# Seven products of quarters in place of eight, for half of K of sixteen products, and a merge that goes branch by branch

## The chip, the core and the metric

The kernel runs on one core of one Trainium2 chip. The metric is the time of one execution on the device, in microseconds (us). The core has a matrix engine (TensorE, PE in the rows), three engines for elementwise work (VectorE, DVE; ScalarE, ACT; GpSimd, POOL) and an engine that here only starts transfers (SyncE, SP). Each works through its own queue in order. They share an on-chip memory of 128 partitions. Matrix products land in PSUM, eight banks of 128x512 numbers of 4 bytes.

## The reference, cut to what is computed

One layer of a decoder for 256 positions and a model width D of 2048, in single precision:

```
h    = rms_norm(x, norm_mix_g)
proj = h @ w_in                # 2048 x 14336: q k v xr gr sc_b sc_c sc_x g_pre
y_a  = attention(q, k, v) @ w_attn_o        # each branch is 1024 wide
y_b  = rg_lru(xr, gr)     @ w_lru_o
y_c  = short_conv(sc_b, sc_c, sc_x) @ w_sc_o
g_a, g_b, g_c = sigmoid(g_pre + gate_b)     # the gates, 3 x 2048 columns
x    = x + (g_a*y_a + g_b*y_b + g_c*y_c) @ w_out
h    = rms_norm(x, norm_mlp_g)
x    = x + square(relu(h @ w_mlp_up)) @ w_mlp_down    # 2048 -> 8192 -> 2048
out  = rms_norm(x, final_g)
```

## The kernel before

**Numbers in two parts.** Each factor of a product is held as `hi`, the number rounded to the format of the matrix engine, and `lo`, the rest. A product is hi times hi, hi times lo and lo times hi, so every 128 rows of K cost three passes.

**Weights.** They come as 552 units of 256 rows of K by 512 columns (512 KB), one for each job. `fetch` (L133) has SP start the transfer into one of RAW = 5 buffers. `in_parts` (L138) has ACT write `hi` (L141) and DVE write `lo` = raw - hi (L142), each 128x1024, into one of WB = 6 slots. `ahead` (L145) is called before each job for the jobs up to LOOK = 3 further on. A slot comes free when PE has finished the job that reads it, so the conversion of a later job begins there.

**Two kinds of product.** `group` (L219) keeps the weights in the array and streams the activations; it serves the projections xr, qk, sc, sx, sb, gr and the first MLP product up. Its chunk is two units, 32 matmuls, of which 16 (L228) stream only 256 columns. `pair` (L247) keeps the activations in the array and streams 512 columns of weights; it serves v, the gates gt, the branch products y, the output projection wo and the second MLP product dn. A pair makes four PSUM tiles, (row tile t, column group i), each 128x512. With K of 2048 it has 16 jobs, two column groups of eight units, and a job is 12 matmuls (2 row tiles, 2 halves of the unit, 3 passes, L266). A pair of dn covers a quarter of K of that product, and its name gives the part and the pair: dn10 is part 1, pair 0. The name gt21 is the third branch, second pair.

**What lies beside.** A generator given to `beside` (the attention, L537; the second norm) emits its next step at each `a_bit` (L209), which `group` calls once per chunk and `pair` once per two jobs. A group or pair leaves the rest of its evacuation in `after`, one piece of which goes out per `a_bit`. `finish` emits all that is left.

**Order.** SP runs in the order of the program. The queues of PE, ACT, DVE and POOL are set by a scheduler when the kernel is built. The list of weights (L104) must be in the order in which the products are called: sc, sx, sb, gr with the attention steps spread over them, one per chunk, then gt and y in turn for three branches, two pairs each, then wo, then four parts of up and dn.

**Buffers.** `block` gives tiles of 128x512 out of NBLK = 59. Six PSUM banks (`bank`) serve groups and pairs, two (`small`) serve transposes and the attention. In the attention each head h makes `lg` (logits), `pp` (transposed weights of the softmax, copied to `pT` by ACT at L561) and `po` (values), and all three take a small bank.

The kernel already has a branch for seven products in `pair` and in `ahead`, but with every NB_ constant at 0 it makes no jobs of that kind.

Of the kernel before, what the change touches and what calls it, by code (L numbers as in the profile page):

```python
# [7 lines left out]
F32 = mybir.dt.float32  # L8
# [4 lines left out]
P = 128  # L13
# [23 lines left out]
NBLK = 59  # L37
RAW = 5
WB = 6
# [4 lines left out]
NB_V = NB_GATE = NB_Y = NB_OUT = NB_DOWN = 0  # L44


def as_sequence(nu, nb):

    n1, n2 = ([("n", 0, 0, i, u) for u in range(4 * nb // 2, nu)] for i in range(2))
    if not nb:  # L50
        return n1 + n2
    s = {m: [("s", m, b, 0, 0) for b in range(nb)] for m in range(1, 8)}
    h = len(n1) // 2
    return s[1] + s[2] + s[3] + n2[:h] + s[4] + n2[h:] + s[5] + n1[:h] + s[6] + n1[h:] + s[7]
# [3 lines left out]
def trunk_kernel(ctx, tc, x8, xn, pv, rows, w_in, rel, onehot, w_a, lru_w, w_l, w_s, w_out, w_up, w_down, out2):  # L58
# [27 lines left out]
    def h_mixed(b, k, m):  # L86
        raise NotImplementedError
# [18 lines left out]
    order += [("ws", w_in, g, 0, 8, 0) for g in (12, 13, 14, 15, 10, 11, 8, 9)]  # L106
    for br, w in enumerate((w_a, w_s, w_l)):
# [86 lines left out]
    side, after = [], []  # L194

# [23 lines left out]
    def group(name, w, g, acts, evac):  # L219

        nk = follow("ws", w, g)
        ps = [bank(f"{name}_{j}") for j in range(4)]
        rest = []

        def block_product(j, k, hi, lo, kk):
            cs = slice(j * P, (j + 1) * P)
            pe.matmul(ps[j], hi[:, kk, cs], acts[k], start=(k == 0), stop=False)  # L227
            pe.matmul(ps[j][:, :S], lo[:, kk, cs], acts[k][:, :S], start=False, stop=(k == nk - 1))  # L228

        for k0 in range(0, nk, 4):  # L230
            u = used[0]
            used[0] += 2
            ahead(u + 1 + LOOK)
            if u < 2:
                for k in range(k0, k0 + 4):
                    for j in range(4):
                        block_product(j, k, *parts[u + (k - k0) // 2], k % 2)
            else:
                for j in range(4):
                    for k in range(k0, k0 + 4):  # L240
                        block_product(j, k, *parts[u + (k - k0) // 2], k % 2)
                    if k0 + 4 == nk:
                        rest.append(evac(j, ps[j]))
            a_bit()
        after.extend(r for r in rest if r)

    def pair(name, w, g, plain, mixed, evac):  # L247


# [20 lines left out]
        def copied(key, what):  # L270
            r = block(f"{name}{what}")
            act.activation(r, ps[key], AF.Copy)
            got[what] = r

        def summed(what):
            r = block(f"{name}{what}")
            dve.tensor_add(r, ps[1, 0], got["r1"])
            got[what] = r

        others = {(0, 0): (None, None), (0, 1): ("x", OP.subtract), (1, 0): ("r1", OP.add), (1, 1): ("z", OP.add)}  # L280
        for n, s in enumerate(seq):
# [10 lines left out]
            else:  # L292
# [3 lines left out]
                if b == nb - 1:  # L296
                    if m == 1:
                        copied((0, 0), "r1")
                    elif m == 2:
                        copied((0, 1), "r5")  # L300
                    elif m == 3:
                        summed("x")
                    elif m == 4:
                        summed("y")
                        z = block(f"{name}z")
                        dve.tensor_sub(z, got["r5"], got["y"])
                        got["z"] = z
# [227 lines left out]
    pair("v", w_in, 4, lambda k, t: in_two(hl[k], t), h_mixed, evac)  # L535
# [76 lines left out]
    for gidx in range(2):  # L612
        def evac(j, ps, gidx=gidx):
            g = 4 * gidx + j
            b = total(ps, f"sb{g}")
            dve.tensor_mul(b, b, rsb)
            dve.tensor_mul(b, b, half(sc, g))
            o = block(f"C{g}", F32R)
            split(o, b)
            C.append(o)  # L620
        group(f"sb{gidx}", w_in, 10 + gidx, hl, evac)


    for gidx in range(2):
        def evac(j, ps, gidx=gidx):
            g = 4 * gidx + j
            y = total(ps, f"gr{g}")

            def rest():
                dve.tensor_mul(y, y, rsb)  # L630
                z = u256(f"gz{g}")
                act.activation(z, y, AF.Square)
                act.activation(z, z, AF.Copy, scale=0.044715, bias=1.0)
                pool.tensor_mul(z, z, y)
                act.activation(z, z, AF.Tanh, scale=math.sqrt(2.0 / math.pi))
                dve.scalar_tensor_tensor(y, z, 1.0, y, op0=OP.add, op1=OP.mult)
                dve.scalar_tensor_tensor(y, half(hh, g), 0.5, y, op0=OP.mult, op1=OP.mult)
                o = block(f"B{g}", F32R)
                split(o, y)
                B.append(o)  # L640
            return rest
        group(f"gr{gidx}", w_in, 8 + gidx, hl, evac)
# [76 lines left out]
    for p2 in range(2):  # L719
# [28 lines left out]
        pair(f"wo{p2}", w_out, 2 * p2, m_plain, None, evac)  # L748
# [16 lines left out]
    for part in range(PARTS):  # L765
        U = []
        for gidx in range(4):
            def evac(j, ps):
                b = total(ps, f"up{part}{gidx}{j}")
                dve.scalar_tensor_tensor(b, b, 0.0, b, op0=OP.max, op1=OP.mult)  # L770
                o = block(f"U{part}{gidx}{j}", F32R)
                split(o, b)
                U.append(o)
            group(f"up{part}{gidx}", w_up, 4 * part + gidx, h2, evac)
# [5 lines left out]
        for p2 in range(2):  # L780
# [12 lines left out]
            pair(f"dn{part}{p2}", w_down, 2 * p2, lambda k, t: in_two(U[k], t), None, evac)  # L793
# [77 lines left out]
```

## Time and profile before

| | |
|---|---|
| median of 3 executions | 1610.56 us (1610.06 to 1612.92) |
| the profiled execution: own time | 1611.42 us |
| the profiled execution: span of the trace | 1609.7 us |
| mean granted clock of TensorE | 0.997 |
| PE busy | 1582.9 us, 98% of the span |
| DVE busy | 958.4 us, 60% |
| ACT busy | 760.8 us, 47% |
| chain of work that ended last | PE 97% |

The busy time of an engine is a sum over stages with different limits, so the shares say which engine to look at, not what a change is worth. For PE the chain of waits gives what the work costs without a gap. For the engines beside it the question is stage by stage whether they are done in time, and for that the timeline of DVE and ACT is read, from the start of one instruction to the start of the next where they stand close.

### The profile page before, as it was taken

The numbers are of one execution on the slowest core, as the hardware profiler recorded it, in microseconds if no ns is written. First come the engines' busy times: TensorE is split into PE (matmuls) and PEld (weight loads), VectorE is DVE, ScalarE is ACT, GpSimd is POOL, SyncE is SP. The second block draws the span as 40 slices with busy tenths as digits, with TensorE's granted clock in tenths as the row PEclk, the third lists the DMA queues.
The fourth block names the chain that finished last, engine by engine and source line by source line (L and its number), as shares of the span: only waits on it lengthen the run. The fifth ranks groups of instructions, "written<-read, shape, count | busy, mean of one in ns | idle before, by whom it ended". The sixth has DMA issues, their size and how long they took to land.

```text
span 1609.7 us, 20538 instructions
## 1 busy us (share of the span) xinstructions
PE 1582.9 (98%) x7886; PEld 1338.5 (83%) x7886; DVE 958.4 (60%) x1237; ACT 760.8 (47%) x1026; POOL 74.8 (5%) x85
## 2 busy tenths in 40 slices
PE   6999999999999999999999999999999999999996
PEld 5888888888888888888888888888888888888885
DVE  8865566776655565555655566555654655556553
ACT  5545845556544444344445554344433444344442
POOL 6021200001100000000000000000000000000000
PEclk9999999999999999999999999999999999999998
DMA  7665465555756665765655556655656556655662
GB/s 256 223 206 168 145 219 170 173 171 183 243 191 195 221 195 192 237 201 184 194 184 185 176 187 196 192 186 186 194 191 209 184 183 200 200 183 184 197 195 65
DMA packets 86418, 307.65 MB, mean 191 GB/s; under 512 B 10141, under 2 KB 10405, under 8 KB 86320
## 3 DMA queue, kind: packets, MB, share of 16 engines
q1 hardware_dynamic: 82656, 296.57, 57.4%
q0 software_dynamic: 2656, 8.45, 1.8%
q10 hardware_dynamic: 1008, 1.32, 0.3%
q8 instruction: 61, 1.00, 0.3%
q14 instruction: 37, 0.30, 0.1%
HBM read 304.20 MB, written 2.11 MB: 190 GB/s over the span
## 4 chain that ended last, share of the span: by engine, by line
PE 97%; DVE 1%; DMA 1%; ACT 0%; issue 0%; ACTq 0%; SPq 0%; DVEq 0%
PE dn L266 22%; PE gt L266 16%; PE up L227 15%; PE y L266 8%; PE up L228 8%; PE wo L266 5%; PE qk L227 4%; PE v L266 3%; PE qk L228 2%; PE sb L227 2%; PE sc L227 2%; PE sx L227 2%; PE gr L227 2%; PE xr L227 1%; PE sc L228 1%; PE sb L228 1%
## 5 line engine op out<-in xcount | busy, mean ns | idle before, releaser
L142 DVE TENSOR_TENSOR lo<-raw,hi 128x1024 fp32r<-128x1024 f32 x552 | 671.8, 1229 | 571.9 <-ACT hi L141 571.7
L141 ACT ACTIVATE hi<-raw 128x1024 fp32r<-128x1024 f32 x552 | 575.3, 1057 | 701.7 <-PE dn L266 193.1
L227 PE MATMUL up<-h,hi 128*128 128x512 f32 x1024 | 362.1, 399 | 0.0
L266 PE MATMUL dn<-hi,U 128*128 128x512 f32 x1024 | 316.2, 389 | 0.0
L228 PE MATMUL up<-h,lo 128*128 128x256 f32 x1024 | 287.9, 281 | 0.0
L266 PE MATMUL gt<-hi,h 128*128 128x512 f32 x768 | 238.0, 390 | 0.0
L227 PEld LDWEIGHTS up<-h,hi 128*128 128x128 f32 x1024 | 192.6, 188 | 47.6
L266 PEld LDWEIGHTS dn<-hi,U 128*128 128x128 f32 x1024 | 192.3, 188 | 40.0
L266 PE MATMUL dn<-lo,U 128*128 128x512 f32 x512 | 199.4, 389 | 0.0
L228 PEld LDWEIGHTS up<-h,lo 128*128 128x128 f32 x1024 | 193.8, 189 | 0.1
L266 PEld LDWEIGHTS gt<-hi,h 128*128 128x128 f32 x768 | 144.2, 188 | 29.9
L266 PE MATMUL gt<-lo,h 128*128 128x512 f32 x384 | 149.5, 389 | 0.0
L266 PEld LDWEIGHTS dn<-lo,U 128*128 128x128 f32 x512 | 96.1, 188 | 19.7
L227 PE MATMUL qk<-h,hi 128*128 128x512 f32 x256 | 91.5, 401 | 0.0
L266 PEld LDWEIGHTS gt<-lo,h 128*128 128x128 f32 x384 | 72.1, 188 | 14.8
L228 PE MATMUL qk<-h,lo 128*128 128x256 f32 x256 | 71.8, 280 | 0.0
L227 PEld LDWEIGHTS qk<-h,hi 128*128 128x128 f32 x256 | 48.1, 188 | 12.1 <-ACT hi L141 0.6
L227 PE MATMUL xr<-h,hi 128*128 128x512 f32 x128 | 46.0, 410 | 7.7 <-DVE h L349 7.6
L266 PE MATMUL wo<-hi,MH 128*128 128x512 f32 x128 | 50.2, 392 | 0.0
L266 PE MATMUL wo<-hi,ML 128*128 128x512 f32 x128 | 49.9, 390 | 0.0
L266 PE MATMUL wo<-lo,MH 128*128 128x512 f32 x128 | 49.8, 389 | 0.0
L228 PEld LDWEIGHTS qk<-h,lo 128*128 128x128 f32 x256 | 48.4, 189 | 0.3
(752 smaller groups left out, 1772.8 us busy)
## 6 DMA issues: line engine op xcount, KB each, us to landing
raw<-in_w_in SPq DMA_DIRECT2D x222, 512.0 KB, 4.3
raw<-in_w_up SPq DMA_DIRECT2D x128, 512.0 KB, 4.0
raw<-in_w_down SPq DMA_DIRECT2D x128, 512.0 KB, 4.2
raw<-in_w_out SPq DMA_DIRECT2D x32, 512.0 KB, 3.6
raw<-in_w_a SPq DMA_DIRECT2D x16, 512.0 KB, 4.4
raw<-in_w_s SPq DMA_DIRECT2D x16, 512.0 KB, 4.3
raw<-in_w_l SPq DMA_DIRECT2D x16, 512.0 KB, 4.3
gb<-in_rows POOLq DMA_DIRECT2D x12, 256.0 KB, 5.0
```

Source lines behind the costliest of these rows:

```text
L141: act.activation(hi, raw, AF.Copy)
L142: dve.tensor_sub(lo, raw, hi.bitcast(F32))
L227: pe.matmul(ps[j], hi[:, kk, cs], acts[k], start=(k == 0), stop=False)
L228: pe.matmul(ps[j][:, :S], lo[:, kk, cs], acts[k][:, :S], start=False, stop=(k == nk - 1))
L266: pe.matmul(ps[key], hl_[x], w2[y][:, kk], start=key not in begun, stop=end and i == 2, skip_group_check=True)
```

## The change

Two constants of `as_sequence` are set: NB_GATE = NB_OUT = NB_DOWN = 2. In the 16 pairs of gt (6), wo (2) and dn (8), units 0 to 3 of K (half of it) are computed by Strassen's scheme: the activations and the weights are cut into quarters, and seven products of sums of quarters replace eight products of quarters. Two blocks b of K, of 512 rows each, share the products' banks. Such a pair has 22 jobs: 14 of kind "s" with 6 matmuls each (products m1 to m7, for b = 0 and 1) and 8 of kind "n" as before. A DVE add in place makes the sum of weight quarters for m2, m3, m4 and m6, and each of the 14 "s" jobs gets its own hi and lo. The sums of activation quarters are made once: for h (`h_sums`, beside the attention), for m (in the rest of gt2/y2, with copies `mf`), and for U of the first two groups of each part (`rest` of up). Products m2, m1, m3 and m4 meet in DVE operations (`step`, L302 and L303) that write two more blocks.

The order of the jobs in a pair is m1, m1, n, m2, m2, n, m3, m3, n, m4, m4, n (of the second column group), then m5, n, m5, m6, n, m6, m7... with the n of the first. A pair uses five banks, since m2 gets its own, (2,0).

The stages are reordered: sc, sx, gt0 and y0, sb, gt1 and y1, gr, gt2 and y2, wo. The attention runs beside sc and sx alone, three steps per `a_bit` (`pace[0] = 3`). `finish` is called before every gate pair and y pair. RAW goes from 5 to 9, WB from 6 to 5, NBLK from 59 to 55.

The number of instructions by queue: PE 7829 before and 7637 after, DVE 1232 and 1696, SP 574 both, POOL 90 both.

```diff
-NBLK = 59
-RAW = 5
-WB = 6
+NBLK = 55
+RAW = 9
+WB = 5
...
-NB_V = NB_GATE = NB_Y = NB_OUT = NB_DOWN = 0
+NB_V, NB_Y = 0, 0
+NB_GATE, NB_OUT, NB_DOWN = 2, 2, 2
...
+    def mixed(ms, ns):
+        ss = [("s", m, b, 0, 0) for m in ms for b in range(nb)]
+        out = []
+        for i, n in enumerate(ns):
+            out += ss[len(ss) * i // len(ns):len(ss) * (i + 1) // len(ns)] + [n]
+        return out
+
+    return mixed((1, 2, 3, 4), n2) + mixed((5, 6, 7), n1)
...
+    def sums(name, a1, a2):
+
+        c = block(f"{name}c")
+        c4 = [c[:, i * P:(i + 1) * P] for i in range(4)]
+        dve.tensor_sub(c4[0], a1[:, P:], a2[:, P:])
+        dve.tensor_sub(c4[1], c4[0], a1[:, :P])
+        dve.tensor_sub(c4[2], a1[:, :P], a1[:, P:])
+        dve.tensor_add(c4[3], a2[:, :P], c4[1])
+        hi, lo = block(f"{name}ch", F32R), block(f"{name}cl", F32R)
+        act.activation(hi, c, AF.Copy)
+        dve.tensor_sub(lo, c, hi.bitcast(F32))
+        return hi, lo
...
-            a_bit()
+            a_bit(pace[0])
...
-        home = {1: (0, 0), 7: (0, 0), 2: (0, 1), 5: (0, 1), 3: (1, 0), 4: (1, 0), 6: (1, 0)}
+        home = {1: (0, 0), 7: (0, 0), 2: (2, 0), 5: (0, 1), 3: (1, 0), 4: (1, 0), 6: (1, 0)}
...
+        def step(m):
+
+            if m == 1:
+                got["r1"] = block(f"{name}r1")
+                act.activation(got["r1"], ps[0, 0], AF.Copy)
+            elif m in (3, 4):
+                o = got["wz"[m - 3]] = block(f"{name}{m}")
+                dve.tensor_add(o, ps[1, 0], got["r1"])
+                dve.tensor_sub(o, ps[2, 0], o)
...
+    beside(h_sums())
...
+    pace[0] = 3
...
+        if before:
+            before()
...
+            finish()
...
-            if br == 0 and p2 == 0:
-                finish()
+            finish()
+            pace[0] = 1
             pair(f"y{br}{p2}", w, 2 * p2, lambda k, t: in_two(acts[k], t), None, evac)
```

The queue of DVE in the first half of the pair dn10, before. The name raw407 is the raw weights of job 407, hi and lo its parts, xr the residual stream:

```order
L142 TENSOR_TENSOR lo407_9907<-raw407_9904,hi407_9906 128x1024
L142 TENSOR_TENSOR lo408_9925<-raw408_9922,hi408_9924 128x1024
L142 TENSOR_TENSOR lo409_9943<-raw409_9940,hi409_9942 128x1024
L142 TENSOR_TENSOR lo410_9961<-raw410_9958,hi410_9960 128x1024
L142 TENSOR_TENSOR lo411_9981<-raw411_9978,hi411_9980 128x1024
L142 TENSOR_TENSOR lo412_10001<-raw412_9998,hi412_10000 128x1024
L787 SCALAR_TENSOR_TENSOR xr00_6786<-dn10_00_9836,rs2_6804,xr00_6786 128x512
L787 SCALAR_TENSOR_TENSOR xr10_6794<-dn10_10_9843,rs2_6804,xr10_6794 128x512
```

The queue of DVE in the first half of dn10, after (job 460 is the pair's first, U133 the last activation of up13):

```order
L159 TENSOR_TENSOR lo463_10326<-raw460_00_10208,hi463_10325 128x1024
L116 TENSOR_TENSOR U131_10287<-up131b_10284,U131_10287 128x256
L116 TENSOR_TENSOR U132_10303<-up132b_10300,U132_10303 128x256
L340 TENSOR_TENSOR up133b_10316<-up13_3_10113,up133a_10314 128x256
L159 TENSOR_TENSOR lo464_10340<-raw461_00_10246,hi464_10339 128x1024
L815 SCALAR_TENSOR_TENSOR up133b_10316<-up133b_10316 128x256
L159 TENSOR_TENSOR lo465_10354<-raw465_10351,hi465_10353 128x1024
L116 TENSOR_TENSOR U133_10319<-up133b_10316,U133_10319 128x256
L186 TENSOR_TENSOR raw460_00_10208<-raw460_00_10208,raw466_11_10371 128x1024
L186 TENSOR_TENSOR raw461_00_10246<-raw461_00_10246,raw467_11_10385 128x1024
L186 TENSOR_TENSOR raw464_01_10336<-raw464_01_10336,raw467_11_10385 128x1024
L159 TENSOR_TENSOR lo466_10375<-raw460_00_10208,hi466_10374 128x1024
```

Where one conversion followed another, adds in place (L186) now stand between them.

The queue of PE in the second half of sx, before, where an attention step stands alone at the head of a chunk:

```order
L228 MATMUL sx1_3_2645<-h7_151,lo91_2649 128x256
L557 MATMUL pp2_2766<-ident_77,lgs20_2510 128x128
L558 MATMUL pp2_2766<-ident_77,lgs21_2519 128x128
L559 MATMUL pp2_2766<-ident_77,lgs21_2519 128x128
L227 MATMUL sx1_0_2642<-h8_164,hi92_2654 128x512
```

The queue of PE in sc, after:

```order
L560 MATMUL lg40_2366<-qk110_1561,qk010_1101 128x128
L560 MATMUL lg41_2375<-qk110_1561,qk010_1101 128x256
L245 MATMUL sc1_0_2244<-h8_164,hi76_2256 128x512
L572 MATMUL pp3_2384<-ident_77,lgs30_2294 128x128
L573 MATMUL pp3_2384<-ident_77,lgs31_2303 128x128
L574 MATMUL pp3_2384<-ident_77,lgs31_2303 128x128
L246 MATMUL sc1_0_2244<-h8_164,lo76_2257 128x256
L245 MATMUL sc1_0_2244<-h9_167,hi76_2256 128x512
L246 MATMUL sc1_0_2244<-h9_167,lo76_2257 128x256
L245 MATMUL sc1_0_2244<-h10_236,hi77_2324 128x512
L581 MATMUL po2_2390<-pT2_2314,vv00_1784 128x256
L582 MATMUL po2_2390<-pT2_2314,vv01_1786 128x128
```

Three steps, of heads 4, 3 and 2, now stand within six matmuls of one chunk, where there was one.

The queue of DVE in the pair gt21, before. The names pm, MH and ML are the transposed merge of four rows of K of wo and its two parts:

```order
L142 TENSOR_TENSOR lo255_6403<-raw255_6400,hi255_6402 128x1024
L699 TENSOR_TENSOR ML0_6334<-pm0_6328,MH0_6333 128x512
L699 TENSOR_TENSOR ML2_6343<-pm2_6337,MH2_6342 128x512
L142 TENSOR_TENSOR lo256_6421<-raw256_6418,hi256_6420 128x1024
L142 TENSOR_TENSOR lo257_6439<-raw257_6436,hi257_6438 128x1024
L699 TENSOR_TENSOR ML4_6388<-pm4_6382,MH4_6387 128x512
L699 TENSOR_TENSOR ML6_6397<-pm6_6391,MH6_6396 128x512
L142 TENSOR_TENSOR lo258_6457<-raw258_6454,hi258_6456 128x1024
```

The queue of DVE in gt21 where its product m3 is read out, after. The name m11c is the last of the sums of m's quarters, gt213 and gt214 are the blocks made from m3 and m4, gt21_10 is the bank in which both are summed:

```order
L186 TENSOR_TENSOR raw278_00_6436<-raw278_00_6436,raw293_10_6761 128x1024
L100 TENSOR_TENSOR m11c_6569<-mf6_6558,m11c_6569 128x128
L186 TENSOR_TENSOR raw279_00_6454<-raw279_00_6454,raw295_10_6792 128x1024
L159 TENSOR_TENSOR lo293_6765<-raw278_00_6436,hi293_6764 128x1024
L103 TENSOR_TENSOR m11cl_6575<-m11c_6569,m11ch_6574 128x512
L159 TENSOR_TENSOR lo294_6777<-raw294_6774,hi294_6776 128x1024
L302 TENSOR_TENSOR gt213_6695<-gt21_10_6677,gt21r1_6605 128x512
L303 TENSOR_TENSOR gt213_6695<-gt21_20_6634,gt213_6695 128x512
L159 TENSOR_TENSOR lo295_6796<-raw279_00_6454,hi295_6795 128x1024
L302 TENSOR_TENSOR gt214_6738<-gt21_10_6677,gt21r1_6605 128x512
```

The read of m3, which the first matmul of m4 waits for, stands behind the sums and behind the conversions of m6 (jobs 293 and 295).

## Rows read from the trace of the kernel before

**Rows 1.** Page, part 1: busy us (share of the span) x instructions.

```profile
PE 1582.9 (98%) x7886; PEld 1338.5 (83%) x7886; DVE 958.4 (60%) x1237; ACT 760.8 (47%) x1026; POOL 74.8 (5%) x85
```

**Rows 2.** Chain that ended last, in order of time: start us, us, what.

```profile
399.96 43.55 PE gt L266 x192
...
976.51 87.06 PE dn L266 x384
1154.02 87.06 PE dn L266 x384
...
1596.13 0.76 DVE xr L787
```

**Rows 3.** Groups of instructions, shapes apart: busy us, mean ns | idle before, releasers.

```profile
L142 DVE TENSOR_TENSOR lo<-raw,hi 128x1024 fp32r<-128x1024 f32 x552 | 671.8, 1229 | 571.9 <-ACT hi L141 571.7
L141 ACT ACTIVATE hi<-raw 128x1024 fp32r<-128x1024 f32 x552 | 575.3, 1057 | 701.7 <-PE dn L266 193.1 <-PE gt L266 141.4 <-PE up L227 90.3
```

**Rows 4.** Windows of a dn and an up stage: us, busy (x) by engine, clock, DMA.

```profile
976.00:1063.00 87.00, 87.00 (x387) 72.07 (x386) 46.09 (x45) 35.57 (x36) 0.00 (x0) 1.00 0.63 196
889.00:976.00 87.00, 87.00 (x497) 75.62 (x495) 53.48 (x82) 44.52 (x70) 0.00 (x0) 1.00 0.55 178
```

**Rows 5.** Timeline of DVE in four places: start us, busy us, instruction.

```profile
265.15 0.29 DVE L547 TENSOR_TENSOR lgs<-lg,tb 128x128 f32<-128x128 f32 x1 [3.57 <-PE lg L545]
265.36 1.22 DVE L142 TENSOR_TENSOR lo<-raw,hi 128x1024 fp32r<-128x1024 f32 x1
...
584.54 1.28 DVE L674 TENSOR_TENSOR gt<-y,gt 128x512 f32<-128x512 f32 x2
...
978.00 0.42 DVE L99 TENSOR_TENSOR U<-up032b,U 128x256 fp32r<-128x256 f32 x1
978.34 0.42 DVE L325 TENSOR_TENSOR up033b<-up,up033a 128x256 f32<-128x256 f32 x1
978.67 1.22 DVE L142 TENSOR_TENSOR lo<-raw,hi 128x1024 fp32r<-128x1024 f32 x1
979.81 0.42 DVE L770 SCALAR_TENSOR_TENSOR up033b<-up033b 128x256 f32<-128x256 f32 x1
...
997.85 1.40 DVE L787 SCALAR_TENSOR_TENSOR xr<-dn,rs,xr 128x512 f32<-128x512 f32 x2
```

**Rows 6.** Timeline of ACT and DVE in dn00: one conversion, with its wait.

```profile
984.73 1.06 ACT L141 ACTIVATE hi<-raw 128x1024 fp32r<-128x1024 f32 x1 [1.66 <-PE dn L266]
...
985.83 1.23 DVE L142 TENSOR_TENSOR lo<-raw,hi 128x1024 fp32r<-128x1024 f32 x1 [1.50 <-ACT hi L141]
```

**Rows 7.** Timeline in sx: transposes of one head on PE, then ACT.

```profile
258.12 2.01 ACT L141 ACTIVATE hi<-raw 128x1024 fp32r<-128x1024 f32 x2 [1.31 <-PE sx L227]
...
258.97 0.27 PE L559 MATMUL pp<-ident,lgs 128*128 128x128 f32 x1
...
260.04 0.47 ACT L561 ACTIVATE pT<-pp 128x384 f32<-128x384 f32 x1
```

**Rows 8.** Windows after PE's last matmul; the column before the DMA share is the granted clock.

```profile
1597.00:1598.00 1.00, 0.00 (x0) 0.00 (x0) 0.81 (x2) 0.64 (x2) 0.00 (x0) 1.00 0.00 0
1599.00:1600.00 1.00, 0.00 (x0) 0.00 (x0) 0.86 (x5) 0.35 (x1) 0.00 (x0) 0.50 0.00 0
```

**Rows 9.** Timeline of PE at its start: the same pair of matmuls, twice at each pace.

```profile
9.68 0.63 PE L227 MATMUL xr<-h,hi 128*128 128x512 f32 x1
...
10.32 0.63 PE L227 MATMUL xr<-h,hi 128*128 128x512 f32 x1
...
11.45 0.40 PE L227 MATMUL xr<-h,hi 128*128 128x512 f32 x1
...
11.80 0.40 PE L227 MATMUL xr<-h,hi 128*128 128x512 f32 x1
```

**Rows 10.** Timeline of DVE at 26.57 us, while POOL squared and added tiles.

```profile
26.57 2.06 DVE L190 TENSOR_TENSOR lo<-raw,hi 128x1024 fp32r<-128x1024 f32 x1
```

**Rows 11.** Page, part 6: transfers of weights, x issues, KB each, us to landing.

```profile
raw<-in_w_in SPq DMA_DIRECT2D x222, 512.0 KB, 4.3
```

More of the change, by code (lines that the diff above doesn't have):

```diff
@@ L105, in trunk_kernel @@
     order.append(("as", w_in, 4, 0, 8, NB_V))
-    order += [("ws", w_in, g, 0, 8, 0) for g in (12, 13, 14, 15, 10, 11, 8, 9)]
-    for br, w in enumerate((w_a, w_s, w_l)):
+    for br, (w, gs) in enumerate(((w_a, (12, 13, 14, 15)), (w_s, (10, 11)), (w_l, (8, 9)))):
+        order += [("ws", w_in, g, 0, 8, 0) for g in gs]
         for pair in range(2):
@@ L194, in trunk_kernel @@
     side, after = [], []
+    pace = [1]
     def beside(gen):
@@ L268, in product @@
                 begun.add(key)
[L270 to L280, printed above, removed]
+        def step(m):
[6 more added lines that the diff above has]
+                dve.tensor_sub(o, ps[2, 0], o)
+        others = {(0, 0): (None, None), (0, 1): ("w", OP.add), (1, 0): ("r1", OP.add), (1, 1): ("z", OP.add)}
         for n, s in enumerate(seq):
@@ L296, in pair @@
                 if b == nb - 1:
[L297 to L307, printed above, removed]
+                    step(m)
             for key in keys:
-                if last[key] == n:
+                if last[key] == n and key in others:
                     o, op = others[key] if nb else (None, None)
@@ L584, in trunk_kernel, with h_sums @@
     beside(attention())
+    hm = {}
+    def h_sums():
+        for b in range(NB_GATE):
+            for kk in range(2):
+                a = block(f"ha{b}{kk}")
+                for i in range(2):
+                    h = hl[4 * b + 2 * i + kk].bitcast(F32)
+                    dve.tensor_add(a[:, i * S:(i + 1) * S], h[:, :S], h[:, S:])
+                hm[b, kk] = sums(f"h{b}{kk}", a[:, :S], a[:, S:])
+                yield
+    beside(h_sums())
+    pace[0] = 3
     sc = []
@@ L611, in trunk_kernel @@
         group(f"sx{gidx}", w_in, 14 + gidx, hl, evac)
[L612 to L642, printed above, removed]
@@ new lines, in second_factor, with evac, recurrent_gate, rest @@
+    def second_factor():
+        for gidx in range(2):
+            def evac(j, ps, gidx=gidx):
+                g = 4 * gidx + j
+                b = total(ps, f"sb{g}")
+                dve.tensor_mul(b, b, rsb)
+                dve.tensor_mul(b, b, half(sc, g))
+                o = block(f"C{g}", F32R)
+                split(o, b)
+                C.append(o)
+            group(f"sb{gidx}", w_in, 10 + gidx, hl, evac)
+    def recurrent_gate():
+        for gidx in range(2):
+            def evac(j, ps, gidx=gidx):
+                g = 4 * gidx + j
+                y = total(ps, f"gr{g}")
+                def rest():
+                    dve.tensor_mul(y, y, rsb)
+                    z = u256(f"gz{g}")
+                    act.activation(z, y, AF.Square)
+                    act.activation(z, z, AF.Copy, scale=0.044715, bias=1.0)
+                    pool.tensor_mul(z, z, y)
+                    act.activation(z, z, AF.Tanh, scale=math.sqrt(2.0 / math.pi))
+                    dve.scalar_tensor_tensor(y, z, 1.0, y, op0=OP.add, op1=OP.mult)
+                    dve.scalar_tensor_tensor(y, half(hh, g), 0.5, y, op0=OP.mult, op1=OP.mult)
+                    o = block(f"B{g}", F32R)
+                    split(o, y)
+                    B.append(o)
+                return rest
+            group(f"gr{gidx}", w_in, 8 + gidx, hl, evac)
@@ L645, in trunk_kernel @@
     acc = {}
-    MH, ML = {}, {}
-    for br, (w, acts) in enumerate(((w_a, A), (w_s, C), (w_l, B))):
+    MH, ML, mm = {}, {}, {}
+    for br, (w, acts, before) in enumerate(((w_a, A, None), (w_s, C, second_factor), (w_l, B, recurrent_gate))):
+        if before:
+            before()
         for p2 in range(2):
@@ L699, in rest @@
                         dve.tensor_sub(ML[n], pm, MH[n].bitcast(F32))
-                return rest
-            if br == 0 and p2 == 0:
-                finish()
+                        if gi < NB_OUT:
+                            mf.append(block(f"mf{n}"))
+                            act.activation(mf[j], pm, AF.Copy)
+                    if gi < NB_OUT:
+                        for kk in range(2):
+                            mm[gi, kk] = sums(f"m{gi}{kk}", *(f[:, kk * S:(kk + 1) * S] for f in mf))
+                return rest
+            finish()
+            pace[0] = 1
             pair(f"y{br}{p2}", w, 2 * p2, lambda k, t: in_two(acts[k], t), None, evac)
@@ L792, in evac @@
                     dve.tensor_mul(o, o, gf[i])
-            pair(f"dn{part}{p2}", w_down, 2 * p2, lambda k, t: in_two(U[k], t), None, evac)
+            pair(f"dn{part}{p2}", w_down, 2 * p2, lambda k, t: in_two(U[k], t), um, evac)
     v2 = const.tile([P, 2], F32, name="v2")
```

45 lines of the change are left out of this document (27 added, 18 removed).

## The prediction

> **What bounds the kernel now.** First the busy shares: PE 98%, no other engine above 60% [rows 1]. Then the chain of waits, followed in time: each gate pair is one piece of PE without a gap, 43.55 us for 192 matmuls, and two dn pairs are another, 87.06 us for 384 [rows 2]. So PE's work is the time, and a matmul of a pair costs 43.55/192 = 226.8 ns; a job "s" of 6 is 1.36 us, a job "n" of 12 is 2.72 us. PE gives up its lead only at 1596.1, when DVE's last results begin [rows 2].
>
> Third, who feeds PE. Every unit's conversion on DVE (552 of them) waits for ACT, and ACT waits for a matmul that frees the slot [rows 3]: both idle because PE is slow. In the window of the two dn pairs DVE is busy 46.1 of 87 us, in the up stage 53.5 of 87 [rows 4]. The change puts its work there, so the question is whether DVE remains the faster one.
>
> Durations are taken from start to start, since the ends overlap: 128x1024 costs 1.14 us (978.67 to 979.81), 128x256 .34, 128x128 .21; two 128x512 took 1.28, with the last end's .08 (1.22 less 1.14) taken off .60 each, and .66 for the form with a scalar [rows 5].
>
> **The sum on PE.** Each of 16 pairs goes from 192 to 14 x 6 + 8 x 12 = 180 matmuls, 12 fewer; 16 x 12 = 192 in all, as the queues' counts say (7829 to 7637). 192 x 226.8 ns = 43.5 us, all of it on the path. That alone gives 1611.4 - 43.5 = 1567.9 on the profiled execution's own clock. Strassen's extra adds land beside PE.
>
> **DVE in a changed pair.** A dn pair needs 22 conversions and 8 adds in place, 30 x 1.14 = 34.2; the four operations on m3 and m4, 4 x .60 = 2.4; four results and three second operands, 7 x .66 = 4.6. That is 41.2 us against PE's 180 x .2268 = 40.8. A gate pair comes to 41.1, a wo pair to 40.8. DVE had a reserve of nearly half; now it has none. It is worse within a pair. The first 12 jobs hold six adds and all work on m3 and m4: DVE 18 x 1.14 + 2.4 + 1.3 = 24.2 us, PE 8 x 1.36 + 4 x 2.72 = 21.8. The other ten: 17.0 against 19.0. Between them stands what was converted ahead, three or four jobs, some 5 us of PE. So a pair that DVE enters on time nearly passes; one that it enters late stops PE by the delay. Once PE frees a slot, ACT's 1.06 and DVE's 1.23 follow [rows 6], so a lo is there at best some 2.4 us after the job that freed its slot.
>
> I added up DVE's queue in the changed order, place by place, against the moment at which PE wants each lo:
>
> - *dn, first pair of each part.* In dn10 lo463 is done about 2.6 us after PE begins the pair (its slot came free at the beginning). Then stand five 128x256 of up and six 128x1024 up to lo466, 5 x .34 + 6 x 1.14 = 8.5, so 11.1; I add .3, an estimate, for starts that wait for a result just made. PE wants it after 4 x 1.36 + 2 x 2.72 = 10.9. Late by .5 to .6 with that, four times: 2.4 us. The second pairs follow a pair that ended level: .5 each in three, and 2.2 in the last, where four products with the final scale are added: 3.7. Together 6.1.
> - *gt00.* Before it the queue holds h's sums (8 x .34 + 4 x (4 x .21 + .60)), the convolution of sx and the conversions. From the attention's last evacuation to lo103, the pair's eighth, it adds up to 49.6 us, plus 2 of waits for slots, and it begins 2 us after the end of a chunk of sc; from that end PE has six chunks of 5.65 us (sixteen in the up stage from 976.51 + 87.06 = 1063.57 to 1154.02 [rows 2]) and 12.2 in the pair, 46.1. Late by 7.5.
> - *gt10, gt20.* The rests of sb and gr stand ahead of their first conversions: 1.6 and 2.9 by the same sum. gt01, gt11 and wo0 come out level, wo1 .2.
> - *gt21.* The second parts of m, its copies and its sums stand in the queue: 4 x .60 for ML and 4 x (4 x .21 + .60) = 8.2 us. They push the read of m3 behind the conversions of m6. The first matmul of m4 uses the same bank and waits: the read comes at about 30.5 us of the pair, where the order of PE has room until 25. PE stands for about 4.7, and with lateness before it this place costs 6.6.
> - *The attention.* Three steps per chunk. The values of one head take the small bank that the transposes of the next left, so they wait for ACT's copy pT. It stands behind two conversions: at 258.12 ACT took up two, 2.01 us, and the copy of transposes that ended at 259.24 began at 260.04 and took .47 [rows 7]. Before, PE had a whole chunk before it needed it; now, six matmuls. I find PE .9 us early five times, and 2.7 us for the first steps: 7 us, with 3 to 12 as bounds (3 if ACT's queue puts the copy first, 12 if every head pays one conversion and the copy, 8 x 1.5).
>
> Sum: 6.1 + 7.5 + 1.6 + 2.9 + .2 + 6.6 + 7 = 31.9.
>
> **The clock.** After PE's last matmul the granted clock was 1.00 (2.4 GHz) for another us and .50 (1.2 GHz) from 1599.0 [rows 8], three us after the end. A stop of 4.7 us in gt21 could reach that; the shorter ones not. No row shows PE working under a granted .50; the nearest slow pace is at its start, where a pair of matmuls took .64 us, then .35 [rows 9], though the clock column reads 1.00 there. Five pairs at that pace cost 5 x .29 = 1.5 us: added once. The Trainium skill (TensorE: Matmul & The Clock Gate, "HAM oscillation") says that an engine which idles too long between groups of matmuls starts the next at half speed; the rows agree that the clock falls, and by the page every long stop, not gt21's alone, would pay.
>
> Transfers cost nothing: no unit is fetched twice, one lands in 4.3 us [rows 11], and nine buffers hold the quarters that stay for several products. POOL gets nothing.
>
> So 1611.4 - 43.5 + 31.9 + 1.5 = 1601.3 by the profiled execution, which lies .9 above the median of the runs: **1600.5**. The bounds of the terms: attention 3 to 12, gt00 4 to 9, gt21 2 to 9, the dn pairs 1 to 12 (no waiting starts, or .8 more in each pair), the small ones 0 to 4.7: 10 to 46.7, that is about 1577 to 1615.
>
> **Rivals.**
> *DVE keeps up.* If the scheduler's order costs little, the stalls shrink to the attention's 3 and some 4 in the gates: 1567 + 7, between 1568 and 1580. For it: DVE's starts overlap, and the deficit in a dn pair is only .4. Against: gt00 and gt21, whose queues are long whatever the pairs do. Chance .10.
>
> *The gain is cancelled.* Stalls of 40 to 46: dn pairs at the 12 end, gates carrying their lateness from one to the next. 1607 to 1616. Chance .18, a sixth of it above 1613.8.
>
> *Slower: the adds in place are dearer than a conversion.* They write the buffer that they read, and ACT and then DVE read that next. Twelve pairs have no slack: two gates and wo0, wo1 and the eight dn, with six adds each in the tight half, 72. Slower than before from (1611.4 - 1601.3)/72 = .14 us more for each, that is 1.28 us; between a start to start of 1.14 and the one conversion that took 2.06 while POOL used the memory too [rows 10], I take 1.14, since in these stages POOL is at 0 [rows 4]. At 1.40, 72 x .26 = 19 more: 1619. Chance .10. The Trainium skill (VectorE: DVE Perf Modes, "The DRAIN you can't avoid") says that an operation starts only when the one ahead has left the pipe; by that each of 30 costs 1.23, not 1.14, 2.7 us a pair more. The starts at 978.67 and 979.81 speak against it.
>
> That the change does not do what it says is no rival: the queues' counts show the fewer matmuls.
>
> **Chances.** The forecast, 1580 to 1607, has .62. A measurement of this kernel tells about 0.2%, so 1607.3 to 1613.8 is no change. Faster .62 + .10 = .72; same .15; slower .03 + .10 = .13. The range 1574 to 1613 leaves out half of the first rival (.05), the slower one (.10) and the top of the second (.03), .18.
>
> **What would show it.** PE's matmuls of a pair still 227 ns, and 12 fewer. PE's idle time, now almost none, some 30 us in: the attention (waits for ACT's pT), gt00 (for lo), gt21 (for the read of m3), and half a us in each dn pair at m3. DVE's share near 100% in gate and dn pairs. Wrong would be: idle PE in the dn pairs of 2 us and more (then the adds or the ends are dearer), a 128x1024 add apart from 1.14, a clock under 1.00 outside gt21, or PE without idle in gt00.

## The result, and the profile after

The changed kernel takes 1594.42 us (median of 4 runs, 1590.80 to 1596.78) against 1610.93 for the kernel before, a ratio of 0.9894 with a 95% interval of 0.9878 to 0.9910. The profiled execution took 1596.78, its span is 1594.7. The forecast was 1600.5, faster.

The page of the profile after, parts 1 and 4, answers [rows 1]:

```profile
PE 1553.9 (97%) x7694; PEld 1302.7 (82%) x7694; DVE 1300.3 (82%) x1701; ACT 873.8 (55%) x1166; POOL 77.0 (5%) x85
...
PE 88%; DVE 7%; issue 2%; ACT 1%; DMA 1%; POOL 1%; SPq 0%; ACTq 0%; DVEq 0%; POOLq 0%
```

DVE went from 60% to 82% busy, and the chain that was PE for 97% is PE for 88% and runs through DVE and ACT for 8%. The chain in order of time (start us, us, what) has these pieces for [rows 2]:

```profile
329.61 28.45 PE gt L291 x123
...
379.82 40.80 PE gt L291 x180
...
757.37 21.59 PE gt L291 x84
...
980.24 81.86 PE dn L291 x360
```

A pair that is not stopped costs 40.80 us for 180 matmuls, 226.7 ns each as before, and two dn pairs 81.86 instead of 87.06. But gt00 and gt21 are no longer one piece: what is left after their last stop has 123 and 84 matmuls.

Where the gain went is read by stage. The table takes each stage from the start of its first matmul to the start of the next stage's, in the timelines of PE before and after; "alone" is the stage before less 2.72 us (12 matmuls) for each changed pair in it.

| stage | before | alone | after | over |
|---|---|---|---|---|
| start, to the end of xr | 63.3 | 63.3 | 65.5 | 2.2 |
| sc, sx, sb, gr with the attention | 193.2 | 193.2 | 194.7 | 1.5 |
| gt00 | 43.5 | 40.8 | 44.8 | 4.0 |
| gt01 and gt11 | 87.0 | 81.6 | 81.6 | 0 |
| gt10 | 43.5 | 40.8 | 41.6 | 0.8 |
| gt20 | 43.5 | 40.8 | 47.4 | 6.6 |
| y20 and gt21 (with 16 transposes) | 67.1 | 64.4 | 72.8 | 8.4 |
| wo | 91.5 | 86.1 | 87.9 | 1.8 |
| dn, parts 0 to 2 | 3 x 87.1 | 3 x 81.7 | 3 x 81.9 | 0.6 |
| dn, part 3 | 87.2 | 81.7 | 84.2 | 2.5 |

The last column adds up to 28.4, and 43.5 - 28.4 = 15.1 is the difference of the spans, 15.0, within rounding. (An expectation below, rounded otherwise, has 28.3, with 1.4 for the attention.) Most of the 2.2 at the start is scatter: in the kernels below, nearly all of which start by the same code as the changed one, xr ends anywhere between 62.9 and 64.9.

The waits of PE after (waited for: us in total, times, longest); the two lines of xr left out here are the start:

```profile
PE gt L291 <- ACT hi L158: 4.5, 7, 1.2
PE gt L291 <- ACT gt21r L299: 4.0, 1, 4.0
PE gt L291 <- DVE lo L159: 2.5, 4, 0.9
PE dn L291 <- ACT hi L158: 1.1, 3, 0.5
PE wo L291 <- DVE lo L159: 0.9, 1, 0.9
PE wo L291 <- ACT MH L729: 0.3, 1, 0.3
```

These six add up to 13.3 us, half of the overruns behind the start. A bracket counts from the end of a matmul, .39 after its start, where the next one would have started after .23, and the lower clock behind a stop is not in it.

Windows after (us, busy (x) of PE, PEld, DVE, ACT, POOL, granted clock, DMA share, GB/s): gt20 and 5 us in it, gt21 and 10 us in it, the first dn stage:

```profile
658.00:706.00 48.00, 44.47 (x186) 35.08 (x185) 45.03 (x56) 30.21 (x43) 6.12 (x6) 0.96 0.57 195
675.00:680.00 5.00, 4.56 (x13) 3.20 (x14) 5.00 (x6) 4.59 (x5) 0.00 (x0) 0.68 0.31 96
728.00:779.00 51.00, 45.93 (x197) 36.52 (x195) 46.32 (x63) 30.17 (x37) 4.26 (x8) 0.93 0.60 206
755.00:760.00 5.00, 2.63 (x6) 2.00 (x7) 4.70 (x6) 2.32 (x4) 0.00 (x0) 0.53 0.45 144
760.00:765.00 5.00, 5.00 (x19) 3.92 (x18) 1.86 (x3) 2.13 (x2) 3.12 (x6) 0.78 0.55 180
980.00:1062.00 82.00, 82.00 (x363) 67.64 (x362) 81.34 (x87) 47.65 (x51) 0.00 (x0) 1.00 0.59 205
```

In the dn stage DVE is busy 81.34 of 82 us and PE does not stop: the two are level. In gt20 and gt21 PE stops, and the granted clock falls behind the stops.

The stop in gt21, from the timelines of PE, ACT and DVE (start us, busy us):

```profile
752.94 0.39 PE L291 MATMUL gt<-hi,h11cl 128*128 128x512 f32 x1
...
757.37 0.80 PE L291 MATMUL gt<-hi,h 128*128 128x512 f32 x1 [4.05 <-ACT gt21r L299]
...
754.32 1.06 ACT L158 ACTIVATE hi<-raw 128x1024 fp32r<-128x1024 f32 x1 [3.18 <-DVE raw L186]
755.28 0.61 ACT L102 ACTIVATE m11ch<-m11c 128x512 fp32r<-128x512 f32 x1
755.80 1.04 ACT L158 ACTIVATE hi<-raw 128x1024 fp32r<-128x1024 f32 x1
756.74 0.58 ACT L299 ACTIVATE gt21r<-gt 128x512 f32<-128x512 f32 x1
...
751.77 0.69 DVE L103 TENSOR_TENSOR m10cl<-m10c,m10ch 128x512 fp32r<-128x512 f32 x1
752.38 0.29 DVE L97 TENSOR_TENSOR m11c<-mf,mf 128x128 f32<-128x128 f32 x1
...
752.98 1.22 DVE L186 TENSOR_TENSOR raw<-raw,raw 128x1024 f32<-128x1024 f32 x1
754.12 0.28 DVE L100 TENSOR_TENSOR m11c<-mf,m11c 128x128 f32<-128x128 f32 x1
...
758.33 0.68 DVE L302 TENSOR_TENSOR gt<-gt,gt21r 128x512 f32<-128x512 f32 x1
```

Read it backwards. PE has done m5 and wants the bank (0,0) for its next job "n"; this bank still holds m1, which ACT copies as gt21r. The copy needs nothing that is late, but ACT works in order, and ahead of it stand three conversions: of a quarter for m6 (754.32), of m's last sums (755.28) and of the weights of an "n" job (755.80). The first waits for DVE's add, which starts at 752.98 because DVE was busy with m's sums and conversions. The last line is the read of m3, for which m4 waits: it comes 29.8 us into the pair, so that PE would soon have stood for it had the copy been early. That is argued from the queue; no run parts the two.

### The profile page after: what moved, and what is told of

Same layout as the page of the kernel before. It is cut to its first block, busy times and chain, and to the rows that moved or that the text cites. A ratio compares the mean times of both kernels' runs of the same rounds, so it can differ in the third digit from the quotient of the medians.

```text
span 1594.7 us, 20814 instructions
## 1 busy us (share of the span) xinstructions
PE 1553.9 (97%) x7694; PEld 1302.7 (82%) x7694; DVE 1300.3 (82%) x1701; ACT 873.8 (55%) x1166; POOL 77.0 (5%) x85
## 4 chain that ended last, share of the span: by engine, by line
PE 88%; DVE 7%; issue 2%; ACT 1%; DMA 1%; POOL 1%; SPq 0%; ACTq 0%; DVEq 0%; POOLq 0%
PE dn L291 20%; PE up L245 15%; PE gt L291 12%; PE up L246 8%; PE y L291 7%; PE wo L291 5%; PE qk L245 4%; PE v L291 3%; DVE lo L159 2%; PE qk L246 2%; PE sc L245 2%; PE sx L245 2%; DVE raw L186 1%; PE sb L245 1%; PE xr L245 1%
## 5 line engine op out<-in xcount | busy, mean ns | idle before, releaser
L159 DVE TENSOR_TENSOR lo<-raw,hi 128x1024 fp32r<-128x1024 f32 x648 | 775.2, 1223 | 229.6 <-ACT hi L158 221.6
L158 ACT ACTIVATE hi<-raw 128x1024 fp32r<-128x1024 f32 x648 | 664.8, 1055 | 533.2 <-DVE raw L186 105.5
L291 PE MATMUL dn<-hi,U 128*128 128x512 f32 x704 | 223.6, 389 | 0.9 <-ACT hi L158 0.9
L291 PE MATMUL gt<-hi,h 128*128 128x512 f32 x528 | 170.4, 394 | 7.1 <-ACT gt21r L299 4.0
L291 PEld LDWEIGHTS dn<-hi,U 128*128 128x128 f32 x704 | 132.0, 188 | 29.0 <-ACT hi L158 1.5
L186 DVE TENSOR_TENSOR raw<-raw,raw 128x1024 f32<-128x1024 f32 x128 | 153.7, 1218 | 0.8
L291 PE MATMUL dn<-lo,U 128*128 128x512 f32 x352 | 137.1, 390 | 0.0
L291 PE MATMUL gt<-lo,h 128*128 128x512 f32 x264 | 103.8, 393 | 0.4 <-DVE lo L159 0.3
L245 PE MATMUL sc<-h,hi 128*128 128x512 f32 x128 | 46.5, 402 | 0.0
L245 PE MATMUL sx<-h,hi 128*128 128x512 f32 x128 | 46.0, 402 | 0.0
```

The lines of the kernel that those rows point to most:

```text
L158: act.activation(hi, raw, AF.Copy)
L159: dve.tensor_sub(lo, raw, hi.bitcast(F32))
L186: dve.tensor_add(t, t, add)
L291: pe.matmul(ps[key], hl_[x], w2[y][:, kk], start=key not in begun, stop=end and i == 2, skip_group_check=True)
```

## The experiments

All edits are to the changed kernel. Comparisons with "after" go by its 1594.42 us, and the ratios by the kernel before, run beside each. Its medians there go from 1609.84 to 1611.29, so a us or two between two of the kernels below says little; what an edit does is read at its place.

**Order alone.** 

> All three NB constants at 0: the new order of stages, the attention at three steps, the buffer counts and the calls of finish stay, every pair is plain again. Theory (each stall belongs to the seven products' own load on DVE and ACT): PE has its 192 matmuls back, and of the 28.3 us by which the changed kernel's stages exceed their matmuls only the start (2.2), the attention (1.4) and a us or two at gr remain: 1611 + 4 to 6, 1615 to 1617. Rival (the order and the calls of finish make the stops at gt20 and gt21): 7 to 15 us over before in those pairs here too, 1620 to 1630.

```diff
-NB_GATE, NB_OUT, NB_DOWN = 2, 2, 2
+NB_GATE, NB_OUT, NB_DOWN = 0, 0, 0
```

Measured: 1612.24 us, ratio 1.0008 (0.9998 to 1.0017). The new order with its attention at three steps costs a us (2.7 at the upper end of the interval), less than either theory had. In its profile PE waits for nothing after xr; gt20 takes 43.6 and y20 with gt21 67.2, as before. So the stops in the table come with the seven products. Of the attention's 1.5 us, .9 stays, and belongs to the order.

**Only dn by seven products.** 

> NB_GATE = NB_OUT = 0: only the eight dn pairs by seven products. Theory: dn keeps its 21.8 us less 3.1 of stops (three parts .2 each, the last 2.5), and gt and wo give up 21.8 us of matmuls and win back the 20 us and more by which gt00, gt10, gt20, gt21 and wo overran: 1592 to 1597, no different from the whole change. Rival (these overruns belong to the order): they remain, and the time is 1605 or more.

```diff
-NB_GATE, NB_OUT, NB_DOWN = 2, 2, 2
+NB_GATE, NB_OUT, NB_DOWN = 0, 0, 2
```

Measured: 1593.44 us, 0.9890 (0.9872 to 0.9907), the same as the whole change. The gates and wo, half of the saved matmuls, bring nothing in this form: 21.8 us gained, about as much given back at their own stops.

**wo plain.** 

> NB_OUT = 0: wo is plain, and with it the copies mf and the sums of m's quarters go. Theory (these sums make the stop of 7.7 us in gt21, and wo itself loses 1.8): 2 x 12 matmuls come back, 5.4 us, and 8 to 9.5 go: 1590 to 1592. Rival (the second parts of m and the conversions fill DVE in gt21 anyway): +5.4 less 1.8, about 1598.

```diff
-NB_GATE, NB_OUT, NB_DOWN = 2, 2, 2
+NB_GATE, NB_OUT, NB_DOWN = 2, 0, 2
```

Measured: 1588.18 us, 0.9857 (0.9841 to 0.9873). y20 with gt21 falls to 64.5, within .1 of its matmuls alone, and the wait for gt21r is gone. Wo by seven products saves 5.4 us and costs 8.3 at another place.

**No adds in place.** 

> The adds in place of weight quarters (128 of 128x1024) are left out, so the seven products use single quarters; all else stays. DVE has 9.1 us less in each changed pair. Theory (PE waits because DVE is full): the overruns of gt00, gt10, gt21, wo and the last dn go nearly whole and gt20's by half, some 18 us of 25: 1574 to 1580. Rival (the stops come from order on ACT, POOL and the banks, not from DVE's load): 5 us or less, 1588 to 1594.

```diff
-                    dve.tensor_add(t, t, add)
+                    add = add
```

This kernel leaves the sums of weight quarters out, so it does not compute the layer. Measured: 1574.72 us, 0.9774 (0.9759 to 0.9790). gt00 and gt10 come to 40.8 and 40.9, gt20 to 41.1, the last dn stage to 81.8. But gt21 stays at 47.6, with this wait:

```profile
PE gt L291 <- ACT gt21r L299: 2.3, 1, 2.3
```

So the adds make nearly all the stops but gt21's: gt20 fell more than expected, gt21 much less. ACT's waits for the adds went with them; the run does not part these from DVE's load. The stop in gt21 has a cause of its own, found with the late sums below.

**Gelu's product on DVE.** 

> The eight products z*y of the gelu (128x256, L665) run on DVE and no longer on POOL. In gt20 (6.6 us over its matmuls) DVE stands still for POOL's chain 1.5 to 2 us and its own operations beside POOL are longer (0.96 for 0.42, 1.42 for 1.21). Theory (the detour over POOL holds DVE's queue up, and the conversions behind it): DVE gains 3 us and pays four products of .34 in gt20, so gt20 falls from 47.4 to 45 or 46 and the time by 1 to 2.5: 1592 to 1593.5. Rival (it is DVE's load alone): gt20 rises by the 1.4, about 1596.

```diff
-                    pool.tensor_mul(z, z, y)
+                    dve.tensor_mul(z, z, y)
```

Measured: 1589.13 us, 0.9866 (0.9849 to 0.9882). gt20 falls from 47.4 to 44.2, more than expected, though DVE has more to do. In the profile after, POOL and DVE at this place:

```profile
660.25 0.96 POOL L665 TENSOR_TENSOR gz<-gz,gr4b 128x256 f32<-128x256 f32 x1 [12.80 <-ACT gz L664]
661.18 1.72 POOL L665 TENSOR_TENSOR gz<-gz,gr5b 128x256 f32<-128x256 f32 x1
...
660.88 1.42 DVE L186 TENSOR_TENSOR raw<-raw,raw 128x1024 f32<-128x1024 f32 x1
662.22 0.96 DVE L667 SCALAR_TENSOR_TENSOR gr4b<-gz,gr4b 128x256 f32<-128x256 f32 x1
...
670.67 0.42 DVE L667 SCALAR_TENSOR_TENSOR gr7b<-gz,gr7b 128x256 f32<-128x256 f32 x1 [1.08 <-ACT gz L666]
```

A product of 128x256 takes POOL 0.96 to 1.72 us. An operation of DVE that is 0.42 by itself takes 0.96 beside it, and at 670.67 DVE stands 1.08 us for the chain through POOL and ACT, with conversions queued behind. About 3 of the 5 us are gt20, and 1.3 of these are the clock, which does not fall there in this run (the run with the late sums, below, has gt20 at 46.1 with the product on POOL and the clock at 1.00). So the detour over POOL costs 2.0. The rest lies in the start (xr ends at 64.8) and the first up stage, which takes 91.6 or 90.0 in profiles of kernels that differ nowhere near it.

**Half of the adds on POOL.** 

> The adds in place for m4 and m6 (4 of 8 in a pair, 128x1024) run on POOL, which is idle in these stages. Theory (DVE's load makes the stops, and POOL's work is free): half of what leaving the adds out gave, 8 to 10 us: 1585. Rival (POOL is slow and holds DVE up while it runs: a product of 128x512 took it 1.2 to 1.4 us, and conversions beside it took 2.06 and adds 1.42): four adds of 2.5 to 3 us in each pair, DVE slower beside them by a half, and hi waits for POOL: no gain, or slower, 1594 to 1620.

```diff
-                    dve.tensor_add(t, t, add)
+                    (pool if m in (4, 6) else dve).tensor_add(t, t, add)
```

Measured: 1638.14 us, 1.0171 (1.0156 to 1.0186): slower than the kernel before. Its groups (busy us, mean ns | idle before, releasers):

```profile
L159 DVE TENSOR_TENSOR lo<-raw,hi 128x1024 fp32r<-128x1024 f32 x648 | 850.6, 1339 | 231.2 <-ACT hi L158 221.4 <-DMA raw<-in_w_in 4.2 <-DMA raw<-in_w_up 3.6
L186 POOL TENSOR_TENSOR raw<-raw,raw 128x1024 f32<-128x1024 f32 x64 | 176.7, 2761 | 1041.4 <-DVE raw L186 718.0 <-DVE lo L159 82.1 <-DMA raw<-in_w_in 77.8
L186 DVE TENSOR_TENSOR raw<-raw,raw 128x1024 f32<-128x1024 f32 x64 | 96.0, 1514 | 0.8
```

POOL's add takes 2761 ns, and DVE's mean add goes from 1218 to 1514, its conversion from 1223 to 1339. DVE was rid of 64 adds (some 77 us busy) and its conversions alone took 75 more. The dn stages grow from 81.9 to about 88.

**h's sums early.** 

> The sums of h's quarters (h_sums) are made beside the first projections, before the recurrence, and no longer after the attention; they need h alone. Theory (DVE's queue ahead of gt00 is full for 49.6 us, of which these sums are 8.5): gt00 goes from 44.8 to 41 or so and the time by 3 to 4 us: 1590.5 to 1591.5. Rival (the convolution of sx and the adds are enough to fill it): 1 us or less.

```diff
     beside(prepare())
 
+    hm = {}
+
+    def h_sums():
...
+    beside(h_sums())
...
     beside(attention())
-    hm = {}
-
-    def h_sums():
...
-    beside(h_sums())
```

Measured: 1592.29 us, 0.9889 (0.9874 to 0.9904), not to be told from after. gt00 falls by 1.4, to 43.4, but sc and sx together grow by as much, from 104.3 to 105.7, with a new wait of 1.5 us for a lo in sc: the stop moved with the work. (v grows too, from 45.6 to 49.2, but only because 16 transposes of the recurrence stand in it now that stood in qk, which is shorter by the same 3.6.)

**m's sums late.** 

> The four sums of m's quarters are made beside the pair y21, no longer ahead of gt21; MH, ML and the copies mf stay where they are, and wo stays by seven products. Theory (the sums in DVE's queue hold the adds of m6, these hold ACT's conversions, and ACT's copy r1 behind these stops PE for 4.0 us): gt21 goes from 50.3 to 43 or 44, and the time to 1587 to 1589. Rival (ML and the copies mf on ACT do it): gt21 stays above 47, 1592 or more.

```diff
-    MH, ML, mm = {}, {}, {}
+    MH, ML, mm, late = {}, {}, {}, []
...
-                        for kk in range(2):
-                            mm[gi, kk] = sums(f"m{gi}{kk}", *(f[:, kk * S:(kk + 1) * S] for f in mf))
+                        def m_sums():
+                            for kk in range(2):
+                                mm[gi, kk] = sums(f"m{gi}{kk}", *(f[:, kk * S:(kk + 1) * S] for f in mf))
+                                yield
+                        late.append(m_sums())
...
             finish()
+            while late:
+                beside(late.pop(0))
             pace[0] = 1
```

Measured: 1583.89 us, 0.9835 (0.9820 to 0.9850). The window of gt21 in this kernel:

```profile
725.30:767.30 42.00, 42.00 (x192) 34.61 (x191) 40.01 (x43) 27.57 (x33) 4.31 (x8) 1.00 0.63 213
```

No stop, no fall of the clock, y20 with gt21 64.5. Of the single edits that leave nothing out this is the strongest, and it settles gt21: four sums of some 5.8 us of DVE, 4 x (4 x .21 + .60), that are not needed before wo, 40 us later, stood ahead of the adds that ACT waited for.

**Rests spread over the gate pairs.** 

> Ahead of a gate pair only the generators beside are emptied; the rests of the stage before (the convolution of sx, the gelu of gr, the transposes of m) go out one at a time during the gate pair, as in the kernel before. Theory (the calls of finish put these rests in one lump ahead of the pair's conversions on DVE): gt00 goes from 44.8 to 42 or 43, gt20 from 47.4 to 43 or 44, gt21 from 50.3 to 46 or less: 8 to 11 us, 1584 to 1587. Rival (DVE has no slack inside a gate pair, so the lump's work costs the same wherever it stands): 3 us or less, 1591 to 1594, with gt00 and gt20 within 1 us of what they are.

```diff
+    def drain():
+        while side:
+            for _ in side.pop(0):
+                pass
...
-            finish()
+            drain()
             pair(f"gt{br}{p2}", w_in, 16 + 4 * GATE[br] + 2 * p2, lambda k, t: in_two(hl[k], t), hm, evac)
```

Measured: 1591.03 us, 0.9883 (0.9866 to 0.9899). gt00 stays at 44.7, y20 with gt21 is 71.3, and gt20 is 46.1 with the clock at 1.00, just as in the run with the late sums, where the rests were not touched. So the rival's time came, 3 us or less, and at the same clock the spreading gains nothing in gt20; that DVE without slack is the reason is argued from this.

**Three and four edits together.** 

> Three edits together: m's sums beside y21, the gelu's product on DVE, and the rests spread over the gate pairs. Theory (they act at separate places): 1594.4 less 10.5 for the sums, and less what is left at gt00 and gt20 once the rests are spread, 5 to 8 (the gelu's gain is among it): 1576 to 1579. Rival (what is taken from one place comes back at the next): 1582 to 1584, no better than the late sums alone.

Measured: 1582.36 us, 0.9831 (0.9817 to 0.9846). 

> The three edits and a fourth: the sums of h's quarters beside sc, ahead of the attention, so that DVE has 13 chunks instead of six between them and gt00. Theory (DVE is 75% busy beside the attention and has room there): gt00 within 1 us of its 40.8, 1 to 3 us under the three edits. Rival (as in the run that put them beside the first projections, the stop moves to where they now stand): the attention's stages grow by what gt00 gives up, no difference.

```diff
-    beside(attention())
...
     beside(h_sums())
+    beside(attention())
```

Measured: 1581.67 us, 0.9825 (0.9810 to 0.9840). (The diff shows the fourth edit alone.) Both beat both kernels, but neither can be told from the late sums alone, as the rivals had it. With the spread rests and the gelu's edit gt20 falls to 43.7 in the first. In the second, with the same two stops of PE (1.82 and .44), it is 45.3, since the clock fell there (0.96 over the stage) and not in the first. With the fourth edit gt00 goes from 44.7 to 43.2, not to within 1 us of 40.8. sx grows from 49.6 to 51.9 and sc shrinks from 54.1 to 52.1, as attention steps moved from one to the other; together they grow by .3, so here the attention did not take back what gt00 gave.

**Final scale of dn30 on POOL**, on top of the three edits. 

> The late sums, the gelu's product on DVE and the spread rests, and of the eight products with the final scale (128x512) the four of the pair dn30 on POOL, so that they leave DVE's queue ahead of dn31. Theory (these four products, 4 x .60 = 2.4 us of DVE, make the last dn stage's 2.5 us): the last dn stage falls from 84.2 to 82.2 or less, and the time by 2 from 1582: 1580. Rival (POOL holds DVE up while it runs, as with the adds, and each product takes it 1.2 to 1.4 us): what DVE saves it loses by slower conversions beside POOL, the last dn stage stays at 84 or grows.

```diff
-                    dve.tensor_mul(o, o, gf[i])
+                    (dve if p2 else pool).tensor_mul(o, o, gf[i])
```

Measured: 1585.73 us, 0.9844 (0.9830 to 0.9857), 3 us slower than without by the medians and 2 by the ratios, whose intervals overlap. At the place it is plain: the last dn stage grows from 84.2 to 86.7. Among its groups:

```profile
L853 POOL TENSOR_TENSOR xr<-xr,gf 128x512 f32<-128x512 f32 x4 | 8.6, 2151 | 75.5 <-ACT sq L852 75.5
```

and in its timeline of PE:

```profile
1534.52 0.80 PE L296 MATMUL dn<-lo,u312ch 128*128 128x512 f32 x1 [2.86 <-DVE lo L159]
```

Each product takes POOL 2151 ns (684 on DVE), and PE then waits 2.86 us for one conversion. That the four products make the 2.5 us of the last stage is thereby not shown: the move brought more than it took away.

## Why the prediction was right

**The gain on PE** was right to the tenth: 180 matmuls at 226.7 ns, 40.80 us, 43.5 in all.

**DVE without reserve** was right: 41 us of DVE in a pair of 40.8, seen as 81.34 busy of 82. The price of an add in place was right too, 752.98 to 754.12 being 1.14 us, so the slower rival fell. By the first sentences of the Trainium skill's "The DRAIN you can't avoid" (VectorE: DVE Perf Modes), adds and conversions would start 1.22 apart; here, as in [rows 5], they do not, and the section itself goes on to say that an operation which is not held starts earlier. That the adds on DVE give back most of what was lost is shown by the run without them, 19.7 us faster.

**The stops**, forecast at 33.4 with the clock, came to 28.4. That is closer than the terms were, which in part is luck: four were too high by 12.8 in all, three too low by 5.6, and the 2.2 of the start were no term of mine. Term by term:

- *Attention:* 7 forecast, 1.5 measured, of which .9 stays without the seven products. The copy does stand behind two conversions, but PE waits for it nowhere in sc and sx as long as the list shows waits (.15 us). What failed is the moment: I let both slots come free at a chunk's end. In the timeline after, two conversions begin .6 us ahead of the next chunk's first attention step (254.94), so the copy ends just when PE wants it:

```profile
254.33 2.01 ACT L158 ACTIVATE hi<-raw 128x1024 fp32r<-128x1024 f32 x2 [1.53 <-PE sc L245]
...
256.42 0.49 ACT L576 ACTIVATE pT<-pp 128x384 f32<-128x384 f32 x1
...
256.96 0.70 PE L581 MATMUL po<-pT,vv 128*128 128x256 f32 x2
```

- *gt00:* 7.5 forecast, 4.0 measured. The queue's own length was right, 51.6 against 51.8 (277.75, where the conversions before the sums begin, to 329.56, where lo103 ends). Its beginning was not, .5 us after the end of a chunk (277.29) and not 2, and PE still had 1.9 us of the attention's last steps, which I had left out.
- *gt10:* 1.6 forecast, .8 measured.
- *gt20:* 2.9 forecast, 6.6 measured. The step that failed is the one that said POOL gets nothing and left it there: the gelu goes through POOL, and in the new order it does so where DVE has no slack. With the clock at 1.00 the stage takes 46.1 with the product on POOL and 44.2 with it on DVE. So 1.3 are the clock, 2.0 the detour over POOL, and the 3.4 that are left stand against the 2.9.
- *gt21:* 6.6 and 1.5 for the clock forecast, 8.4 measured, at the right place and by the right queue, m's sums. The wait that ended last was not the read of m3, though this came when forecast (29.8 us into the pair; 30.5 forecast), but ACT's copy of m1, behind the conversion that waits for the add.
- *wo:* .2 forecast, 1.8 measured, one stop of .9 for a lo among it; gone to .5 without adds.
- *dn:* 6.1 forecast, 3.1 measured. Three parts cost .2 each and not 1.1: no wait of PE shows in them. I take it that what was converted ahead covered DVE's deficit and that the .3 added for starts that wait was too much; no run tests this. The last part's 2.5 met its 2.8.

**The clock** fell at the forecast place, and at one more. Behind the stop of 4.05 us it was 0.53 and 0.78, which by PE's busy time there is 2.63 x .47 + 5 x .22 = 2.3 us; behind four stops of .4 to 1.2 us in gt20 it was 0.68, 4.56 x .32 = 1.5. I had excluded the second: a clock under 1.00 outside gt21 was one of my signs of being wrong, and it came. The Trainium skill (TensorE: Matmul & The Clock Gate, "HAM oscillation") counts the slow clock behind a wait as a cost beside the wait itself, and this trace agrees, with 2.3 us behind the 4.05.

Yet short stops do not settle it. In the run with the late sums PE makes the same four in gt20 (1.03, .88, 1.19 and .44 us; 1.01, .88, 1.19 and .44 in the changed kernel). There the clock stays at 1.00, and the stage is 1.3 us shorter. The stage and the same 5 us in it, in that run:

```profile
656.00:704.00 48.00, 44.46 (x191) 34.84 (x190) 46.21 (x58) 31.24 (x45) 6.16 (x6) 1.00 0.59 200
673.00:678.00 5.00, 4.55 (x18) 3.36 (x19) 5.00 (x6) 4.70 (x5) 0.00 (x0) 1.00 0.29 80
```

What decides between the two is not shown.

Forecast and median differ by 6.1 us. Of these 4.5 lie between the profiled execution, 1596.8, and the sum's 1601.3; the rest is that this execution lies 2.4 above its kernel's median, while that of before lay .9 above. The changed kernel also spreads more from run to run, 6 us against 3.

## What to carry to other kernels

When a change takes work from the engine that bounds and gives some to one beside it, add up the second engine's queue in its new order against the moments at which the first wants each result; the pairs where it was entered on time kept the whole gain, and the stages that met it with a backlog gave theirs back. Work that nobody needs yet (here the sums for wo) belongs behind the work that is waited for: moving it was worth some 10 us (8.3 at its place), more than the 5.4 that the product it serves saved. An engine that works in order holds up what is ready behind what is not, so look along the queue ahead of the instruction that is late and not at its inputs.

## What the runs showed of the hardware

GpSimd was no free helper for VectorE here. An add of 128x1024 took it 2761 ns against 1218 on VectorE, a product of 128x512 took 2151 against 684, and VectorE's own operations were longer beside it, the add 1514 ns in the mean. An engine at 5% looked like spare room, and giving it 64 adds cost 44 us. (Single spans on POOL are rough in a profile; the 44 us are not.)

TensorE's granted clock can fall behind several stops of about a us as behind one of 4, and the same stops need not bring it down each time: in gt20 they did in the changed kernel and did not with the late sums, a difference of 1.3 us between two profiles of the same work.
